# An encoder block planned at build time: turns on SBUF, table loads and a GpSimd delay enter the planner, and GpSimd adds the fourth square of the first head group

## The chip, the cores and the metric

The kernel runs on one core of a Trainium2 chip. A core has five engines with instruction queues of their own: TensorE (PE in the profile), VectorE (DVE), ScalarE (ACT), GpSimd (POOL) and SyncE (SP). They share an on-chip memory, SBUF; matmul results go to PSUM, of which the kernel uses eight banks. The metric is the device time of one execution in microseconds. The batch is 1, the sequence 512, the model width 1024, all in float32.

## The reference

One layer of a streaming encoder. The part that matters here is the mixer: one projection, two groups of eight heads of width 64, each group normalised by itself, and one output projection.

```python
h = rms_norm(x, g_mix_pre)
q_f, k_f, v_f, f_logit, q_c, k_c, v_c = split(h @ w_in)
log_f = log_sigmoid(f_logit + b_fgate)
# group A, forgetting attention: logit[t,s] = q_t.k_s / 8 + c_t - c_s, c = cumsum(log_f), s <= t
o_f = fox_attention(q_f, k_f, v_f, log_f)
# group B: a 64-token chunk sees itself and the 8 chunks before, with a learned relative bias
o_c = chunked_rel_attention(q_c, k_c, v_c, rel_bias)
o_f = rms_norm(o_f.reshape(B, S, 512), g_fox_out)      # over the whole group
o_c = rms_norm(o_c.reshape(B, S, 512), g_chunk_out)
x = x + rms_norm(concat([o_f, o_c]) @ w_out, g_mix_post)
x = x + rms_norm(memory_cross_attention(rms_norm(x), rms_norm(mem)), g_mem_post)
x = x + rms_norm(swiglu(rms_norm(x), w_gate_up, w_down), g_ffn_post)
```

## The kernel before

Every float32 product is made of three passes (`mm3`, lines L410, L411, L413 by the kind of pass): an operand is split into a rounded part `hi` and the rest `lo`. For a weight block, ACT casts it to `hi` (L392) and DVE subtracts to get `lo` (L393): 128 partitions x 1024 elements, both inputs in SBUF. Raw blocks come in on SP's DMA queue.

**Stages.** First the normalisation statistics and the value projections (to 30 us), then the heads, 16 of them in four groups `n` = 0 to 3 (`n` 0 and 1 are side 0, the FoX group A; 2 and 3 are side 1, the chunked group B), beside the projections of the next groups, the first half of the output projection (tile `mix`) and the products of the memory tokens (to 260 us), then cross-attention (to 390 us) and the feed-forward part (to the end).

**One head** runs over four query blocks of 128, the i-th with (i+1) x 128 keys (`head`): two score matmuls (L796, L797) into a PSUM bank `ps_s`; DVE adds the bias and takes the row's bound in one custom instruction (L800, two records in the profile, in the order of instructions `ISA`); ACT takes the exponential and sums it (L810); DVE makes the reciprocal (L811) and scales the row `p` (L812, one input, in SBUF); PE transposes `p` into a bank `ps_t` (L815); ACT rounds the transposed block to `pth` (L817) and DVE subtracts to get `ptl` (L818). At a head's end PE multiplies with the values (L824). Names in the text: `p5_2` is head 5, block 2, written `p_2` with a number in the order of instructions.

**A pair of heads** fills one tile `o`, 128 x 512. `pair_out` scales and splits it on ACT (`oh`, L836) and DVE (`ol`, L837), and GpSimd squares it: the first pair of a group into a tile `sq` (L841), the later ones in place (L843) with an add into `sq` (L845), except the last pair of the group, whose square stays a tile of its own. `group_rs` then sums over the partitions with one-column matmuls (L851), four per tile of squares, and rstd follows on DVE (L856, L417) and GpSimd (L418). GpSimd also masks the FoX biases (L767), adds the squares of the memory tokens (L888) and issues a few DMAs.

**What sets the order.** All instructions of the stages above up to the feed-forward part are recorded first, and then `planned_order` puts them in a fixed order per engine. It simulates each engine with a duration for each instruction (`duration`), a delay from one engine's end to another's start (`SIGNAL`, `TO_PE`, `LANDED`), the dependences, and the buffers of each tile's tag; whenever an engine comes free, the instruction that has the best priority of those that can start is taken. `later(n)` shifts that priority, and `urge` holds such shifts for the four head groups. The rest of the kernel is in the order in which it is written. In the planner as it is, engines touch each other by dependences alone: nothing is held up by another engine's use of a memory, and an `ACT_TABLE_LOAD`, which the compiler puts ahead of an activation whose function is not in the table at hand, costs nothing.

In cross-attention the probabilities of a head are transposed, cast by ACT (`pt`, L1085) and split by DVE (L1086) before PE multiplies them with the values (`ps_o`). After the last head an activation with Silu on one column (L1100) loads the table that the feed-forward part needs; the weight blocks of the output product are cast around it (`woh`, L392).

Of the kernel before, what the change touches and what calls it, by code (L numbers as in the profile page):

```python
# [10 lines left out]
AF = mybir.ActivationFunctionType  # L11
# [24 lines left out]
ENGINES = mybir.EngineType  # L36
# [5 lines left out]
    (ENGINES.DVE, ENGINES.Pool): 80.0, (ENGINES.Activation, ENGINES.Pool): 67.0,  # L42
    (ENGINES.Pool, ENGINES.DVE): 36.0, (ENGINES.Pool, ENGINES.Activation): 34.0,
}
TO_PE, LANDED = 350.0, 60.0


def number(dims):
    n = 1
    for d in dims:  # L50
        n *= d[1]
    return n
# [37 lines left out]
def planned_order(tc, instructions, homes):  # L90
# [35 lines left out]
    def duration(i):  # L126
        kind = type(i).__name__
        n = number(list(i.outs[0].bass_ap.ap)[1:])
        read = [number(list(a.bass_ap.ap)[1:]) for a in i.ins if tile_of(a)]
        columns = sum(n > 8 and m == 1 for m in read)  # L130
        if i.engine == ENGINES.PE:
            return MATMUL * n + 2.0 if n > P else NARROW
        if i.engine == ENGINES.Activation:
            return (284.0 if len(i.outs) > 1 else 160.0) + 0.838 * n + 80.0 * columns
        if i.engine == ENGINES.Pool:
            if n <= 8:
                return 174.0 if kind == "InstTensorCopy" else 1450.0 if n == 1 else 1040.0
            if kind == "InstTensorTensor" and tile_of(i.ins[0]) != tile_of(i.ins[1]):
                return 25.0 + 4.1 * n
            return 25.0 + (0.96 if kind == "InstMemset" else 2.0) * n  # L140
        if kind == "InstCustomDveAnt":
            return 245.0 + 0.99 * n
        if kind == "InstTensorReduce":
            return 158.0 + 1.02 * read[0]
        if kind == "InstMemset":
            return 70.0 + 0.8 * n
        if kind == "InstReciprocal" or n < 8:
            return 158.0
        full = [a for a in i.ins if tile_of(a) and number(list(a.bass_ap.ap)[1:]) > 8]
        if len(full) < 2 and not any(map(in_psum, full)):  # L150
            return 213.0 + 0.526 * n
        return 150.0 + 1.046 * n + 60.0 * columns

    def halves(i):
        starts = []
        for a in [i.outs[0]] + list(i.ins):
            ap = getattr(a, "bass_ap", None)
            if ap is not None and ap.ap[0][1] >= 8:
                whole = number([(0, n) for n in list(ap.tensor.shape)[1:]]) if tile_of(a) else 0
                starts.append(ap.offset // whole if whole else 0)  # L160
        return (starts + starts + [0, 0])[:2]

    nodes = [i for i in instructions if type(i).__name__ not in ("BassTilePoolBoundary", "InstRegisterMove")]
# [38 lines left out]
    for line in after:  # L202
        for k in line:
            missing[k] += 1

    ready, at = {}, [0.0] * len(nodes)
    for k, i in enumerate(nodes):
        if not missing[k]:
# [3 lines left out]
    def reached(e, other, transfer):  # L212
        if e == other and not transfer:
            return 20.0 if e == ENGINES.PE else -20.0
        return TO_PE if other == ENGINES.PE else LANDED if transfer else SIGNAL.get((e, other), 40.0)

    def may_start(k):
        t = at[k]
# [18 lines left out]
    while any(ready.values()):  # L237
        best = None
        for e, waiting in ready.items():
            starts = [(t, k) for t, k in ((may_start(k), k) for k in waiting) if t is not None]  # L240
            if not starts:
                continue
            now = max(free.get(e, 0.0), min(starts)[0])
            able = [(k, t) for t, k in starts if t <= now + 1.0]
            if e == ENGINES.PE:
                alike = [x for x in able if narrow[x[0]] == after_narrow and (after_narrow or x[1] <= now)]
                late = [x for x in able if narrow[x[0]] and x[1] + patience[x[0]] <= now]
                able = alike if after_narrow and alike else late or alike or able
            if best is None or (now, str(e)) < best[:2]:
                best = now, str(e), e, *min(able)  # L250
        _, _, e, k, t = best
        ready[e].remove(k)
        i, start = nodes[k], max(free.get(e, 0.0), t)
        transfer = type(i).__name__ == "InstDMACopy"
        if transfer:
            free[e] = start + ISSUE
            end = landed[e] = max(start + 1900.0, landed.get(e, 0.0)) + 4 * number(i.outs[0].bass_ap.ap) / 300.0
            if e == ENGINES.Pool:
                end += 1500.0
        elif e == ENGINES.PE:  # L260
            cost = duration(i) + (0.0 if narrow[k] or not after_narrow else SUMMED if summed else TURNED)
            after_narrow, summed = narrow[k], number(list(i.outs[0].bass_ap.ap)[1:]) <= 8
            waited = t > free.get(e, 0.0) + 5.0 and cost > 100.0
            free[e] = start + cost + (95.0 if waited else 0.0)
            end = start + max(cost, 60.0) + 170.0
        else:
            if halves(i) != place.get(e, [0, 0]):
                start = max(start, ends.get(e, 0.0) + 28.0)
            place[e] = halves(i)
            end = ends[e] = start + duration(i)  # L270
            free[e] = max(start + 20.0, end - TAIL[e])
        order.setdefault(e, []).append(i)
        for name in used[k]:
            if name not in lasts:
                lasts[name] = {}
                room[homes.tiles[name]].pop(0)
            lasts[name][e, transfer] = end
            uses[name] -= 1
            if not uses[name]:
                room[homes.tiles[name]].append(name)  # L280
        for j, in_turn in after[k].items():
            other = nodes[j].engine
            at[j] = max(at[j], start if in_turn else (start if e == other == ENGINES.PE else end) + reached(e, other, transfer))
            missing[j] -= 1
            if not missing[j]:
                ready.setdefault(other, []).append(j)
# [15 lines left out]
def hybrid_block_kernel(  # L302
# [195 lines left out]
    with tc.tile_pool(name="mix", bufs=1, reuse_waits="tile") as bp:  # L498
# [374 lines left out]
        sqs = []  # L873
        rs_g = []
        order = [(0, g) for g in fox_order] + [(1, 0), (1, 1)]
        for n, (side, g) in enumerate(order):
            with later(-20):
                q, kt, kl, v = group_proj(f"{side}{g}")
            if n == 3:
                mT = big.tile([P, 2, KB, NMEM], F32R, tag="sB", name="mT")  # L880
                mm = bp.tile([P, KB, NMEM], F32, tag="V", name="mm", bufs=2)
                nc.gpsimd.dma_start(mm, mem_t.rearrange("(k p) n -> p k n", p=P))
                msq = bp.tile([P, 4, NMEM], F32, tag="T", name="msq", bufs=3)
                for k in range(0, KB, 2):
                    b = msq[:, 2 * (k > 0) : 2 * (k > 0) + 2, :]
                    act.activation(b, mm[:, k : k + 2, :], AF.Square, scale=1.0 / 32.0)
                    if k:
                        pool.tensor_tensor(out=msq[:, 0:2, :], in0=msq[:, 0:2, :], in1=b, op=ALU.add)  # L888
            if n == 0:
                gate = forget_gate()  # L890
                oh = ox.tile([P, 8, SEQ], F32R, tag="x1", name="oh")
                ol = ox.tile([P, 8, SEQ], F32R, tag="x2", name="ol")
            if n % 2 == 0:
                sqs.append([bp.tile([P, SEQ], F32, tag="sq", name=f"sq{side}", bufs=1)])
            if n == 2:
                with later(300):
                    rs_g.append(group_rs(sqs[0], "rsg0"))
            for b in range(2):
                pr = 2 * g + b
                o = bp.tile([P, SEQ], F32, tag="o", name=f"o{side}{pr}", bufs=2)  # L900
                for h in range(2):
                    hh = 2 * pr + h
                    if n == 3 and 2 * b + h == 1:
                        mem_norm()
                    with later(urge[n] - 295):
                        bias = fox_bias(hh, *gate) if side == 0 else chunk_bias(hh)
                    with later(urge[n]):
                        head(q[b], kt[b], kl[b], v, 2 * b + h, h, bias, o)
                with later(urge[n]):
                    pair_out(  # L910
                        o, (G_FOX, G_CHK)[side] + pr, oh[:, 4 * side + pr, :], ol[:, 4 * side + pr, :],
                        sqs[side][0], n % 2 == 0 and b == 0, n % 2 == 1 and b == 1,
                    )
                if n % 2 == 1 and b == 1:
                    sqs[side].append(o)

        mix = big.tile([P, NT, D], F32, tag="sA", name="mix")
# [899 lines left out]
```

## Time and profile before

| | |
|---|---|
| median of 3 runs | 757.11 us (757.09 to 757.48) |
| profiled execution | 757.56 us, of which the span of the profile 755.8 |
| PE busy | 744.0 us, 98% of the span, 5032 instructions |
| DVE busy | 603.1 us, 80% |
| ACT busy | 445.3 us, 59% |
| GpSimd busy | 59.3 us, 8%, 101 instructions |

The profile times every instruction of one execution. The median is of three executions without it, so an argument made in the profile's numbers is made against 757.56, and 0.45 is between that and the median. A busy PE can still be slow, but here its granted clock is full throughout, so what is lost on PE shows as gaps between its matmuls.

### The profile page before, as it was taken

To read this page: it belongs to the slowest core of one execution; us is meant where nothing else is said; L and a number is where in the kernel's file an instruction comes from. 1 tells how busy PE (TensorE), PEld (TensorE's weight loads), DVE (VectorE), ACT (ScalarE), POOL (GpSimd) and SP (SyncE) were. 2 spreads that over 40 slices of the span, in tenths; PEclk is the share of its full clock that TensorE was granted. 3 is DMA by queue.
4 is the path that set the end of the run, shared out by engine and by line. 5 is a ranking of instruction groups with operands and counts; after the bars stand their busy time and mean duration, and the time that the engine had idled before them with its cause. 6 is when DMAs were issued, how large, how long until landed. Compare 5 with 4: busy or idle time off the path is not lost.

```text
span 755.8 us, 12990 instructions
## 1 busy us (share of the span) xinstructions
PE 744.0 (98%) x5032; PEld 679.8 (90%) x5032; DVE 603.1 (80%) x1101; ACT 445.3 (59%) x817; POOL 59.3 (8%) x101
## 2 busy tenths in 40 slices
PE   9999999999999999999999999999999999999996
PEld 9988887898789988888878999999999999999995
DVE  8669999798788688445654698999989999998756
ACT  8569998686776458344554445666555557544321
POOL 1001232102201211000001200000000000000001
PEclk9999999999999999999999999999999999999999
DMA  7623233324214725411440023333333322243223
GB/s 254 168 81 97 73 88 112 112 71 144 67 57 138 277 75 181 137 57 56 142 145 21 29 97 105 110 110 112 113 112 112 112 85 84 84 139 113 85 84 111
DMA packets 62204, 82.16 MB, mean 109 GB/s; under 512 B 2872, under 2 KB 44344, under 8 KB 62144
## 3 DMA queue, kind: packets, MB, share of 16 engines
q1 hardware_dynamic: 60432, 76.34, 31.8%
q0 software_dynamic: 1280, 4.72, 1.8%
q8 instruction: 39, 0.64, 0.3%
q10 hardware_dynamic: 432, 0.29, 0.1%
q14 instruction: 21, 0.17, 0.1%
HBM read 79.22 MB, written 2.11 MB: 108 GB/s over the span
## 4 chain that ended last, share of the span: by engine, by line
PE 89%; ACT 5%; DVE 3%; issue 1%; DMA 1%; POOL 0%; POOLq 0%; DVEq 0%; ACTq 0%
PE ps_a L410 13%; PE ps_a L411 13%; PE ps_a L413 13%; PE ps_t L1400 3%; PE ps_t L1397 3%; PE ps_t L1398 3%; PE ps_s L1398 3%; PE ps_s L1400 3%; PE ps_s L1397 3%; PE ps_s L410 3%; PE ps_s L413 3%; PE ps_s L411 3%; PE ps_o L824 2%; PE ps_t L815 2%; PE ps_a L1400 1%; PE ps_a L1397 1%
## 5 line engine op out<-in xcount | busy, mean ns | idle before, releaser
L393 DVE TENSOR_TENSOR lo<-raw,hi 128x1024 fp32r<-128x1024 f32 x56 | 69.9, 1258 | 21.1 <-ACT hi L392 13.8
L413 PE MATMUL ps_a<-hTh,lo 128*128 128x512 f32 x192 | 76.2, 397 | 0.0
L411 PE MATMUL ps_a<-hTl,hi 128*128 128x512 f32 x192 | 76.2, 397 | 0.0
L410 PE MATMUL ps_a<-hTh,hi 128*128 128x512 f32 x192 | 75.8, 395 | 0.0
L392 ACT CAST hi<-raw 128x1024 fp32r<-128x1024 f32 x56 | 57.5, 1047 | 30.3 <-PE ps_a L411 20.4
L1193 DVE TENSOR_TENSOR ring_lo<-sums,ring_hi 128x1024 fp32r<-128x1024 f32 (+1 forms) x39 | 46.6, 1195 | 11.8 <-ACT ring_hi L1192 7.2
L1192 ACT CAST ring_hi<-sums 128x1024 fp32r<-128x1024 f32 (+1 forms) x39 | 40.2, 1030 | 16.5 <-PE ps_s L1398 16.5
L1192 ACT CAST ring_hi<-fraw 128x1024 fp32r<-128x1024 f32 (+1 forms) x26 | 26.5, 1032 | 33.6 <-DVE fraw L1279 17.5
L810 ACT ACTIVATE p<-p,nm 128x128 f32<-128x128 f32 (+1 forms) x64 | 36.0, 562 | 11.1 <-DVE nm L800 10.4
L413 PEld LDWEIGHTS ps_a<-hTh,lo 128*128 128x128 f32 x192 | 36.1, 188 | 6.5
L411 PEld LDWEIGHTS ps_a<-hTl,hi 128*128 128x128 f32 x192 | 36.1, 188 | 6.2
L410 PEld LDWEIGHTS ps_a<-hTh,hi 128*128 128x128 f32 x192 | 36.2, 188 | 6.2
L1193 DVE TENSOR_TENSOR ring_lo<-fraw,ring_hi 128x1024 fp32r<-128x1024 f32 (+1 forms) x26 | 30.9, 1199 | 11.3 <-ACT ring_hi L1192 11.3
L818 DVE TENSOR_TENSOR ptl<-ps_t,pth 128x128 fp32r<-128x128 f32 (+1 forms) x64 | 30.4, 483 | 1.7 <-ACT pth L817 1.5
L817 ACT CAST pth<-ps_t 128x128 fp32r<-128x128 f32 (+1 forms) x64 | 26.7, 420 | 8.3 <-PE ps_t L815 7.7
L815 PE MATMUL ps_t<-ident,p 128*128 128x128 f32 x160 | 28.1, 273 | 2.0 <-DVE p L812 2.0
L812 DVE TENSOR_SCALAR p<-p,rc 128x128 f32<-128x128 f32 (+1 forms) x64 | 28.3, 442 | 0.1
L1398 PE MATMUL ps_a<-b,ring_hi 128*128 128x256 f32 x92 | 25.5, 277 | 0.0
L815 PEld LDWEIGHTS ps_t<-ident,p 128*128 128x128 f32 x160 | 19.8, 140 | 6.4 <-issue 1.7
L1397 PE MATMUL ps_a<-b,ring_hi 128*128 128x256 f32 x92 | 25.5, 277 | 0.0
L1400 PE MATMUL ps_a<-b,ring_lo 128*128 128x256 f32 (+1 forms) x93 | 25.5, 276 | 0.0
L410 PE MATMUL ps_a<-hi,oh 128*128 128x512 f32 x64 | 25.3, 396 | 0.0
(572 smaller groups left out, 2774.6 us busy)
## 6 DMA issues: line engine op xcount, KB each, us to landing
raw<-in_dram SPq DMA_DIRECT2D x64, 512.0 KB, 3.7
fraw<-in_dram SPq DMA_DIRECT2D x26, 512.0 KB, 3.5
place<-in_dram SPq DMA_DIRECT2D x21, 512.0 KB, 4.3
more_room<-in_dram SPq DMA_DIRECT2D x15, 512.0 KB, 4.0
row<-gate_rows SPq DMA_DIRECT2D x8, 256.0 KB, 3.2
cb<-in_dram SPq DMA_DIRECT2D x8, 256.0 KB, 2.6
xo<-in_dram POOLq DMA_DIRECT2D x4, 512.0 KB, 7.5
rawv<-in_dram SPq DMA_DIRECT2D x3, 520.0 KB, 6.3
```

Source lines behind the costliest of these rows:

```text
L392: act.copy(hi[:, j : j + n, :], raw)
L393: dve.tensor_tensor(out=lo[:, j : j + n, :], in0=raw, in1=f32(hi[:, j : j + n, :]), op=ALU.subtract)
L410: pe.matmul(dst, sh, mh, start=first, stop=False)
L411: pe.matmul(dst, sh, ml, start=False, stop=False)
L413: pe.matmul(dst[:, to], sl, mh[:, to], start=False, stop=last)
L810: act.activation(p[:, :n], p[:, :n], AF.Exp, bias=nm, scale=-1.0, accum_out=sm)
L815: pe.transpose(tp[:, k * P : (k + 1) * P], p[:, k * P : (k + 1) * P], ident)
L1192: act.copy(h2, v)
L1193: dve.tensor_tensor(out=l2, in0=v, in1=f32(h2), op=ALU.subtract)
L1397: pe.matmul(dst, w[0][:, k, :], b[:, 0, k, :], start=first and k == 0, stop=False, skip_group_check=more)
L1398: pe.matmul(dst, w[0][:, k, :], b[:, 1, k, :], start=False, stop=False, skip_group_check=more)
L1400: pe.matmul(dst[:, to], w[1][:, k, :], b[:, 0, k, to], start=False, stop=last and k == 3, skip_group_check=more,)
```

## The change

Four things change in the planner, and one in the kernel. `TO_PE`, the delay from an engine's end to PE's start, becomes 900 ns for GpSimd (350 before, as for the others still). An activation whose function is Exp, Ln or Silu, and not the last of these three used, starts 1283 ns later. GpSimd's operation on two tiles is taken as 25 + 2.46 ns per element (4.1 before; at 512 elements 1285 ns for 2124). DVE and GpSimd take turns: an instruction of either with 64 or more elements and no large input in PSUM (`shares`) ends later by what is left of the other engine's last such instruction.

In the kernel, the last pair of side 0 is no longer left out of the add: its square is added to `sq0` by GpSimd like those before, and `group_rs` sums one tile of squares for group A, not two. Group B is as it was.

```diff
-TO_PE, LANDED = 350.0, 60.0
+TO_PE, LANDED = {ENGINES.Pool: 900.0, ENGINES.DVE: 350.0, ENGINES.Activation: 350.0}, 60.0
+TABLES = (AF.Exp, AF.Ln, AF.Silu)
+HOLDS = {ENGINES.DVE: 140.0, ENGINES.Pool: 170.0}
...
             if kind == "InstTensorTensor" and tile_of(i.ins[0]) != tile_of(i.ins[1]):
-                return 25.0 + 4.1 * n
+                return 25.0 + 2.46 * n
...
+    def shares(i):
+        n = number(list(i.outs[0].bass_ap.ap)[1:])
+        return n >= 64 and not any(in_psum(a) for a in i.ins if tile_of(a) and number(list(a.bass_ap.ap)[1:]) >= 64)
+
+    table = [AF.Exp]
+    alone, port = [i.engine in HOLDS and shares(i) for i in nodes], {}
...
-        return TO_PE if other == ENGINES.PE else LANDED if transfer else SIGNAL.get((e, other), 40.0)
+        return TO_PE.get(e, 350.0) if other == ENGINES.PE else LANDED if transfer else SIGNAL.get((e, other), 40.0)
...
             place[e] = halves(i)
+            if getattr(i, "func", None) in TABLES and i.func != table[0]:
+                start, table[0] = start + 1283.0, i.func
             end = ends[e] = start + duration(i)
+            if e in HOLDS and alone[k]:
+                end = ends[e] = end + max(0.0, max(port.get(x, 0.0) for x in HOLDS if x != e) - start)
+                port[e] = end - HOLDS[e]
             free[e] = max(start + 20.0, end - TAIL[e])
...
                     pair_out(
                         o, (G_FOX, G_CHK)[side] + pr, oh[:, 4 * side + pr, :], ol[:, 4 * side + pr, :],
-                        sqs[side][0], n % 2 == 0 and b == 0, n % 2 == 1 and b == 1,
+                        sqs[side][0], n % 2 == 0 and b == 0, n == 3 and b == 1,
                     )
-                if n % 2 == 1 and b == 1:
+                if n == 3 and b == 1:
                     sqs[side].append(o)
```

The added lines put the kernel's body 13 lines lower: L812 is L825 in the changed kernel, L851 is L864. The planner's new numbers move several hundred instructions by a few places. Three places are shown; in each the rows are one engine's instructions in order.

The first place is in head 5, at 101 us. `p_2_1232` is its block 2, `ps_t_1240` the bank that takes its transposes, `ps_a` a projection. DVE before:

```order
L812 TENSOR_SCALAR p_1_1216<-p_1_1216,rc_1219 128x256
L393 TENSOR_TENSOR lo_1583<-raw_0_1584,hi_1582 128x1024
L811 RECIPROCAL rc_1235<-sm_1234 128x1
L818 TENSOR_TENSOR ptl_407<-ps_t_1224,pth_406 128x2x128
L812 TENSOR_SCALAR p_2_1232<-p_2_1232,rc_1235 128x384
L800 ISA p_3_1249,nm_1250<-ps_s_1246,row_1177 128x512
```

DVE in the changed kernel:

```order
L825 TENSOR_SCALAR p_1_1216<-p_1_1216,rc_1219 128x256
L406 TENSOR_TENSOR lo_1584<-raw_0_1585,hi_1583 128x1024
L831 TENSOR_TENSOR ptl_407<-ps_t_1224,pth_406 128x2x128
L824 RECIPROCAL rc_1235<-sm_1234 128x1
L813 ISA p_3_1249,nm_1250<-ps_s_1246,row_1177 128x512
L813 ISA nm_1250 128x1
L825 TENSOR_SCALAR p_2_1232<-p_2_1232,rc_1235 128x384
```

The bias step of block 3 has come ahead of the scaling of block 2. PE before, around the transposes of that block:

```order
L413 MATMUL ps_a_1645<-hi_1098,hTl 128x256
L815 MATMUL ps_t_1240<-ident,p_2_1232 128x128 x3
L410 MATMUL ps_a_1645<-hi_1098,hTh 128x256
L411 MATMUL ps_a_1645<-lo_1099,hTh 128x256
L413 MATMUL ps_a_1645<-hi_1098,hTl 128x256
L796 MATMUL ps_s_1312<-T_1135,Q_1061 128x256
L797 MATMUL ps_s_1312<-L_420,Q_1061 128x256
```

PE in the changed kernel:

```order
L426 MATMUL ps_a_1646<-hi_1098,hTl 128x256
L809 MATMUL ps_s_1312<-T_1135,Q_1061 128x256
L810 MATMUL ps_s_1312<-L_420,Q_1061 128x256
L423 MATMUL ps_a_1646<-hi_1098,hTh 128x256
L828 MATMUL ps_t_1240<-ident,p_2_1232 128x128 x3
L424 MATMUL ps_a_1646<-lo_1099,hTh 128x256
```

The transposes have gone from row 554 of PE's list to row 569, behind twelve more projection matmuls, the next score pair and one matmul more.

The second place is the group sum of group A, at 141 us. `o_1379` is the last pair of that group, `sq_618` the tile of squares. GpSimd before:

```order
L782 MEMSET cb_2113 64x64
L843 TENSOR_TENSOR o_1379<-o_1379 128x512
L418 TENSOR_TENSOR rsg_1862<-rsg_1862,mhalf 128x4
L782 MEMSET cb_2479 64x64
L782 MEMSET cb_2581 64x64
```

GpSimd in the changed kernel:

```order
L795 MEMSET cb_2110 64x64
L856 TENSOR_TENSOR o_1379<-o_1379 128x512
L858 TENSOR_TENSOR sq_618<-sq_618,o_1379 128x512
L431 TENSOR_TENSOR rsg_1859<-rsg_1859,mhalf 128x4
L795 MEMSET cb_2476 64x64
```

PE before, the last two of the seven one-column matmuls and what follows:

```order
L851 MATMUL ps_t_1851<-ones,sq_618 128x1
L851 MATMUL ps_t_1851<-ones,o_1379 128x1
L411 MATMUL ps_a_1816<-hTl,hi_1698 128x512
L413 MATMUL ps_a_1816<-hTh,lo_1699 128x512
L796 MATMUL ps_s_1869<-T_1809,Q_1735 128x256
```

PE in the changed kernel, at its one-column matmuls:

```order
L426 MATMUL ps_a_2206<-hi_1773,hTl 128x256
L423 MATMUL ps_a_2206<-hi_1773,hTh 128x256
L864 MATMUL ps_t_1852<-ones,sq_618 128x1 x4
L424 MATMUL ps_a_2206<-lo_1774,hTh 128x256
L426 MATMUL ps_a_2206<-hi_1773,hTl 128x256
```

GpSimd has one add more; PE's matmuls are four instead of eight, at row 786 of its list. Before, one stood at row 703 and seven at rows 741 to 747, right after the projection into the bank `ps_a_1816`; now the four follow the next score pairs and 40 matmuls of the next projection.

The third place is the end of cross-attention, at 377 us. ACT before:

```order
L1067 ACTIVATE xp_4140,xsm_4185<-ps_s_4171,xnm_4184,mix_rs 128x256 x2
L1085 CAST pt<-ps_t_4162 128x2x256
L1100 ACT_TABLE_LOAD
L1100 ACTIVATE mix_ms<-xsm_4185 128x1
L392 CAST woh<-raw_6_4250 128x1024
L1085 CAST pt<-ps_t_4192 128x2x256
L1095 CAST oT_3645<-ps_o_4201 128x512
```

ACT in the changed kernel:

```order
L1080 ACTIVATE xp_4137,xsm_4182<-ps_s_4168,xnm_4181,mix_rs 128x256 x2
L1098 CAST pt<-ps_t_4159 128x2x256
L1113 ACT_TABLE_LOAD
L1113 ACTIVATE mix_ms<-xsm_4182 128x1
L1098 CAST pt<-ps_t_4189 128x2x256
L405 CAST woh<-raw_6_4247 128x1024
L1108 CAST oT_3642<-ps_o_4198 128x512
```

The last cast of `pt` has gone ahead of the weight cast; the table load stays where it was.

Of the places not shown, four are spoken of below. At 124 us DVE's scaling of p8_0 goes ahead of two subtractions L818. At 198 to 202 us the transposes of p13_1 go behind a score matmul and three 512-wide matmuls, those of p13_2 behind three. Near 230 us the second half of a weight subtraction L393 goes ahead of the output's L837, and the score matmul of block 2 of head 16 goes behind the transposes of p15_3. Near 40 us the steps of the forget gate's scan and copy come a few places later on DVE and PE; on SP the loads of one FoX row and two chunk biases move by one place, and on GpSimd the power of the second group's rstd goes ahead of the copies and DMAs of `xo`, the residual.

## The prediction

> **What bounds the kernel now.** I read the page first (engine busy times, the chain that ended last), then the waits of TensorE, then the windows around each wait, and last the timelines of the engines named there.
>
> ```profile
> PE 744.0 (98%) x5032; PEld 679.8 (90%) x5032; DVE 603.1 (80%) x1101; ACT 445.3 (59%) x817; POOL 59.3 (8%) x101
> PE 89%; ACT 5%; DVE 3%; issue 1%; DMA 1%; POOL 0%; POOLq 0%; DVEq 0%; ACTq 0%
> ```
>
> TensorE (PE) is busy for 744.0 of 755.8 us, and the chain that ended last runs over it for 89%. So an edit is worth what it takes from PE's own list or from PE's few stalls. PE's waits, all of them of 0.2 us or more:
>
> ```profile
> PE ps_t L815 <- DVE p L812: 2.0, 3, 0.9
> PE ps_t L509 <- DVE ones L347: 1.1, 1, 1.1
> PE ps_o L410 <- ACT pt L1085: 0.8, 1, 0.8
> PE ps_s L796 <- DVE nm L800: 0.7, 1, 0.7
> PE ps_t L851 <- POOL o L843: 0.2, 1, 0.2
> ```
>
> All but L509 (the start) lie in the planned part, and windows show how local they are (second number: PE busy, of 10 us; then weight loads, DVE, ACT, POOL):
>
> ```profile
> 100.00:110.00 10.00, 9.14 (x70) 8.56 (x69) 9.92 (x31) 8.83 (x23) 1.86 (x4) 1.00 0.48 132
> 120.00:130.00 10.00, 9.38 (x50) 7.45 (x49) 9.43 (x28) 8.71 (x20) 3.36 (x7) 1.00 0.32 100
> 190.00:200.00 10.00, 9.47 (x45) 7.45 (x44) 7.66 (x16) 9.16 (x19) 2.58 (x2) 1.00 0.35 108
> 230.00:240.00 10.00, 9.28 (x74) 8.90 (x73) 9.76 (x26) 6.89 (x15) 0.54 (x1) 1.00 0.45 153
> 376.00:386.00 10.00, 9.18 (x43) 7.15 (x42) 4.14 (x8) 4.37 (x8) 0.00 (x0) 1.00 0.48 146
> ```
>
> The granted clock is 1.00 in all five, so a lost tenth there is a wait and no slower matmul.
>
> **Stall 1, at 101.** The next fence holds rows of the DVE, POOL and PE timelines (start, duration, in brackets the idle time before) and the group row of L393 (min/median/max).
>
> ```profile
> 98.25 0.35 DVE L812 TENSOR_SCALAR p<-p,rc 128x256 f32<-128x256 f32 x1
> 98.84 2.25 DVE L393 TENSOR_TENSOR lo<-raw,hi 128x1024 fp32r<-128x1024 f32 x1 [0.24 <-ACT hi L392]
> 101.41 0.40 DVE L812 TENSOR_SCALAR p<-p,rc 128x384 f32<-128x384 f32 x1
> ...
> 98.72 1.29 POOL L845 TENSOR_TENSOR sq<-sq,o 128x512 f32<-128x512 f32 x1
> ...
> 100.71 0.28 PE L411 MATMUL ps_a<-lo,hTh 128*128 128x256 f32 x1
> 100.83 0.28 PE L413 MATMUL ps_a<-hi,hTl 128*128 128x256 f32 x1
> 101.97 0.52 PE L815 MATMUL ps_t<-ident,p 128*128 128x128 f32 x3 [0.86 <-DVE p L812]
> ...
> L393 DVE TENSOR_TENSOR lo<-raw,hi x56: 1198/1220/2304, 20.2 to 368.4; 128x1024 fp32r<-128x1024 f32 x56
> ```
>
> GpSimd's add of squares starts at 98.72, a DVE subtraction with both inputs in SBUF starts 0.12 later and takes 2.25 instead of 1.22: it stood for 1.03 of the add's 1.29. The scaling of p (L812) queued behind it, and the transposes behind that. PE's starts lie 1.14 apart (100.83 to 101.97) where a 256-wide matmul takes 0.12 (100.71 to 100.83): the stall costs 1.02, that is the 0.86 of the bracket and 0.16 more. I add the same 0.16 to the other brackets.
>
> **Stalls 2, 4 and 5** have the same cause with other victims; stall 5 is the 2.3 us L393 again.
>
> ```profile
> 123.50 1.10 DVE L812 TENSOR_SCALAR p<-p,rc 128x128 f32<-128x128 f32 x1
> ...
> 123.15 1.28 POOL L845 TENSOR_TENSOR sq<-sq,o 128x512 f32<-128x512 f32 x1
> ...
> 124.75 0.30 PE L815 MATMUL ps_t<-ident,p 128*128 128x128 f32 x1 [0.62 <-DVE p L812]
> ...
> 198.43 1.47 DVE L812 TENSOR_SCALAR p<-p,rc 128x256 f32<-128x256 f32 x1
> ...
> 198.45 1.29 POOL L888 TENSOR_TENSOR msq<-msq 128x512 f32<-128x512 f32 x1 [0.78 <-ACT msq L886]
> ...
> 199.95 0.44 PE L815 MATMUL ps_t<-ident,p 128*128 128x128 f32 x2 [0.53 <-DVE p L812]
> ...
> 229.32 2.30 DVE L393 TENSOR_TENSOR lo<-raw,hi 128x1024 fp32r<-128x1024 f32 x1
> ...
> 229.26 1.28 POOL L845 TENSOR_TENSOR sq<-sq,o 128x512 f32<-128x512 f32 x1
> ...
> 232.04 0.41 PE L796 MATMUL ps_s<-T,Q 128*128 128x384 f32 x1 [0.72 <-DVE nm L800]
> ```
>
> An L812 of 256 columns took 0.35 at 98.25 and 1.47 at 198.43 beside GpSimd. With 0.16 each the three stalls are 0.78, 0.69 and 0.88.
>
> **Stall 3 (140.7) and stall 6 (379.9)** are of another kind:
>
> ```profile
> 139.12 1.54 POOL L843 TENSOR_TENSOR o<-o 128x512 f32<-128x512 f32 x1 [7.63 <-DVE ol L837]
> ...
> 139.94 0.39 PE L413 MATMUL ps_a<-hTh,lo 128*128 128x512 f32 x1
> 140.16 0.39 PE L410 MATMUL ps_a<-hTh,hi 128*128 128x512 f32 x1
> 140.72 0.38 PE L851 MATMUL ps_t<-ones,o 128*128 128x1 f32 x2 [0.16 <-POOL o L843]
> 142.30 0.48 PE L411 MATMUL ps_a<-hTl,hi 128*128 128x512 f32 x1
> ...
> 376.30 0.58 ACT L1085 CAST pt<-ps_t 128x512 fp32r<-128x512 f32 x1
> 376.90 1.28 ACT L1100 ACT_TABLE_LOAD   x1
> 378.19 0.20 ACT L1100 ACTIVATE mix_ms<-xsm 128x1 f32<-128x1 f32 x1
> 378.30 1.03 ACT L392 CAST woh<-raw 128x1024 fp32r<-128x1024 f32 x1
> 379.24 0.58 ACT L1085 CAST pt<-ps_t 128x512 fp32r<-128x512 f32 x1
> 379.87 0.50 PE L410 MATMUL ps_o<-pt,vm 128*128 128x512 f32 x1 [0.82 <-ACT pt L1085]
> ```
>
> In stall 3 PE, which starts a 512-wide matmul every 0.22 to 0.23 (139.94, 140.16), waits 0.16 + 0.16 = 0.32 for the last square, then issues seven of the eight one-column matmuls of the group (the first stands alone earlier): (142.30 - 140.72) / 7 = 0.226 each. In stall 6 the table load of 1.28 delays ACT, the weight cast L392 comes up first, and the cast of pt that PE waits for stands behind it: 0.82 + 0.16 = 0.98.
>
> **The change, part by part** (lines of before; in the changed kernel all these are 13 higher).
>
> *Group sum.* Four of eight L851 matmuls go: 4 x 0.226 = 0.90 off PE's own list, with nothing to hide it. In exchange GpSimd makes one more add, 1.28 (its row at 123.15), with the row of L851 now behind it. Is that late? The multiply started at 139.12; stalls 1 and 2 and one L851 now gone from ahead of it put it near 137.1; 1.54 + 1.28 give 139.9; if one subtraction L393 takes its turn first, 141.1; two, 142.4. PE reaches the four matmuls after 40 256-wide ones (0.117 each, 4.7) and two score pairs (4 x 0.117 = 0.5) behind the place that it reached at 140.39 before, and 2.0 earlier: 143.6. The margin is 1.2 to 3.7, so the 0.32 goes too, and GpSimd's 900 ns to PE is inside it. DVE's L856 now waits for those matmuls with all of head 9's softmax queued behind it: it is free near 144.6, p9_0 needs, by my estimate from L812's 0.35 and the operations like it, 2 us more, and PE has 26 matmuls (3 us) before its transposes.
>
> *Turns on SBUF, and the shorter add.* Stall 1: the add and the L393 still collide, I take the 2.25 as staying. But the transposes stand 15 matmuls later (15 x 0.117 = 1.75), so PE comes to them at about 102.7. On DVE the order is now L818, L800, L812, which puts p some 0.6 later than 101.81, with 0.16 to PE: 102.6. Gone, with 0.1 to spare. Stall 2: L812 goes ahead of the 0.69 subtraction L818, hence to about 122.9, before the add at 123.15. Gone. Stall 4: the transposes move behind 3 x 0.227 + 0.117 = 0.80 of matmuls, against 0.69. Gone, by 0.1. Its neighbour, a 0.2 wait for the next p at 202.1, I leave standing. Stall 5: the second half of L393 goes ahead of the output's L837, whose result starts GpSimd, and the score matmul goes eight rows later, behind the transposes of p15_3. Gone. What is late next there: the add then meets the first L393 of the next weights. If GpSimd issues first, DVE gives p16_0 about 1.2 later than otherwise, against some 0.7 of cover: 0 to 0.9 lost; I take 0.45, since the two starts are too close to call.
>
> *Table load in the plan.* The cast of pt goes ahead of L392. It would run from 378.3 to 378.9, the second half of it on DVE (L1086) follows 0.7 later; PE's first matmul on it would come at 378.9 as before the stall. Up to 0.1 may remain; stall 6 goes. The displaced weight half is read on PE some 30 512-wide matmuls later (30 x 0.22 = 6.6), so its delay of 0.6 is hidden.
>
> The Trainium skill, "ScalarE: Activation LUTs", section "What ACT_TABLE_LOAD costs", prices a switch of tables at about 2.7 us with a drain of 1.4 beside the load. By that rule pt would be 1.4 later and the sum below 1.0 higher; the rows here speak against it, since the load starts 0.02 after the cast before it ends and the next ACTIVATE follows 0.01 after the load. I give it 3 in 100, inside the forecast's range.
>
> *Everything else that moved* (the gate's scan and copy, the first biases, loads of row3, cb3 and cb6 by one place on SP's queue, rsg1's power ahead of the four xo loads on GpSimd's queue): I cost it at nothing. The first biases have the whole projection before the first head as cover, and xo is read only after the output projection's first blocks. If such a cover failed, the price would be of the order of one wait above, 0.3 to 1.0. I add 0.3 for one of them, or for one of the two 0.1 margins.
>
> *Sum.* 1.02 + 0.78 + 0.32 + 0.69 + 0.88 + 0.98 = 4.67, and 0.90: 5.57 off the profiled execution's 757.56 (its span 755.8, 1.8 around it), 751.99. Back come 0.45 + 0.3: 752.7. That execution is 0.45 above the median of the runs, 757.11, so the median comes to 752.3. About 0.2% (1.5 us) is what a measurement can tell from no change.
>
> **The rivals.** *A: DVE stays the limit where it is full.* DVE is busy 9.92 and 9.43 of 10 in the windows of stalls 1 and 2, and 9.76 in that of stall 5. Moving PE's work cannot speed it up; where the add still blocks it, the lost time turns up behind another p. Then only the table load, the four matmuls and stall 3's 0.32 hold: 0.98 + 0.90 + 0.32 = 2.2, time 754.9 (754.0 to 756.5). Against it: of DVE's time in these windows about 1.0, 0.8 and 1.1 are the blocked part itself, and PE has projection matmuls to put in between.
>
> *B: The waits only move.* As A, and the new add brings one collision of its own of 1.28 with its 0.16: 2.2 - 1.4 = 0.8, time 756.3 to 757.1, no change that can be told.
>
> *C: Slower: fillers run out.* The plan spends projection matmuls earlier as cover for late transposes. If the last heads before 250 then stand without any, each quarter of a head brings a wait like those above, which mean (1.02 + 0.78 + 0.69 + 0.88) / 4 = 0.84. It decides at nine bare quarters (7.6 against 5.57 + 1.5): 757.1 - 5.6 + 7.6 = 759.1. The order speaks against it: in the changed kernel 256-wide matmuls still stand between all transposes of heads 15 and 16.
>
> **How the numbers follow.** The forecast, most covers hold, 0.64, with its own range of 751.0 (nothing comes back, and small waits such as that at 202.1 go too) to 753.7 (three covers miss by 0.3 to 0.9). A 0.20, B 0.08, C 0.08. Faster by over 0.2%, below 755.6, is the forecast and most of A: 0.79; within 0.2% the rest of A and B: 0.13; slower 0.08. The range goes from 751.0 to 755.6 and leaves out C, B and the slow end of A.
>
> **What the profile of the changed kernel would show.** Waits: "ps_t <- DVE p" down from 2.0 to 0.5 or less, the rows for pt and nm gone, none for the group sum. Windows: PE at 9.8 or more in 100 to 110 and in 120 to 130, and 9.9 in 376 to 386. The one-column group of squares with half the records for the first group, L845 five times at 1.28. L393 may still show 2.3: then the gain came from the new places of the transposes and not from fewer collisions. I am wrong if PE shows new brackets of over 0.5 in 100 to 250 (A or B), above all for p16_0, or a row of them before 250 (C).

## The result, and the profile after

The changed kernel takes 750.68 us (median of 4 executions, 750.3 to 751.43), the kernel before on the same chip 757.3: a ratio of 0.9913, 95% interval 0.9896 to 0.993. The forecast of 752.3 had the direction and the larger part of the size (4.8 below the 757.11 that it started from, where 6.6 came); its range of 751.0 to 755.6 begins 0.3 us too high. The profiled execution is the fastest of the four (750.3, span 748.5), and that of before one of its slower ones, so the two spans differ by 7.3 where the medians differ by 6.6.

The page of the changed kernel, busy times and the chain that ended last:

```profile
PE 740.4 (99%) x5024; PEld 679.0 (91%) x5024; DVE 602.4 (80%) x1101; ACT 445.1 (59%) x817; POOL 63.4 (8%) x102
PE 98%; issue 0%; DVE 0%; DMA 0%; ACT 0%; POOLq 0%; POOL 0%; DVEq 0%; ACTq 0%
```

The chain runs over PE for 98% of the span, before for 89%. PE has eight records less (a one-column matmul is two). All of PE's waits that the view lists, and three of its windows:

```profile
PE ps_t L522 <- DVE ones L360: 1.0, 1, 1.0
PE ps_s L423 <- DVE vhi L568: 0.4, 1, 0.4
...
100.00:110.00 10.00, 10.00 (x71) 9.29 (x70) 9.80 (x28) 9.18 (x23) 2.23 (x4) 1.00 0.49 132
120.00:130.00 10.00, 10.00 (x54) 8.48 (x53) 9.79 (x27) 9.82 (x23) 3.88 (x8) 1.00 0.39 96
230.00:240.00 10.00, 10.00 (x83) 9.74 (x83) 8.37 (x19) 5.60 (x11) 0.00 (x0) 1.00 0.45 148
```

Both waits are at the start, in the first 6 us. In the planned part none is left: PE is busy for all of the windows in which it lost 0.86, 0.62 and 0.72 before. In the first two DVE is as full as it was (9.80 and 9.79 of 10, before 9.92 and 9.43), so a full DVE did not hold PE up there.

Is the collision gone? The DVE, GpSimd and PE timelines of the changed kernel at the place of stall 1:

```profile
98.72 2.24 DVE L406 TENSOR_TENSOR lo<-raw,hi 128x1024 fp32r<-128x1024 f32 x1 [0.25 <-ACT hi L405]
101.88 0.41 DVE L825 TENSOR_SCALAR p<-p,rc 128x384 f32<-128x384 f32 x1
...
98.59 1.28 POOL L858 TENSOR_TENSOR sq<-sq,o 128x512 f32<-128x512 f32 x1
...
102.22 0.28 PE L809 MATMUL ps_s<-T,Q 128*128 128x256 f32 x1
102.58 0.49 PE L828 MATMUL ps_t<-ident,p 128*128 128x128 f32 x3
```

It is not. The subtraction takes 2.24 beside the add, as before; p is ready at 102.29, and PE comes to the transposes only at 102.58, with no bracket. At 227 us the same two meet in the other order:

```profile
227.10 1.35 DVE L406 TENSOR_TENSOR lo<-raw,hi 128x1024 fp32r<-128x1024 f32 x1 [0.42 <-ACT hi L405]
...
226.16 1.22 POOL L856 TENSOR_TENSOR o<-o 128x512 f32<-128x512 f32 x1 [22.20 <-DVE ol L850]
227.45 2.16 POOL L858 TENSOR_TENSOR sq<-sq,o 128x512 f32<-128x512 f32 x1
```

Here DVE's instruction was first, and GpSimd's add took 2.16 instead of 1.28. No instruction waits for that add. The adds of before and of the changed kernel (min/median/max) show that this is not the only one:

```profile
L845 POOL TENSOR_TENSOR sq<-sq,o x4: 1282/1288/1293, 98.7 to 229.3; 128x512 f32<-128x512 f32 x4
L858 POOL TENSOR_TENSOR sq<-sq,o x5: 1284/2153/2212, 98.6 to 227.4; 128x512 f32<-128x512 f32 x5
```

Three of the five adds now take 2.15 to 2.21, each behind a DVE subtraction that started first. The prediction expected five of 1.28. So in part the new order lets GpSimd bear the collision, and for its adds nobody waits.

### The profile page after: what moved, and what is told of

The parts are those of the page before. It is cut to its first block, busy times and chain, and to the rows that moved or that the text cites. A ratio compares the mean times of both kernels' runs of the same rounds, so it can differ in the third digit from the quotient of the medians.

```text
span 748.5 us, 12983 instructions
## 1 busy us (share of the span) xinstructions
PE 740.4 (99%) x5024; PEld 679.0 (91%) x5024; DVE 602.4 (80%) x1101; ACT 445.1 (59%) x817; POOL 63.4 (8%) x102
## 4 chain that ended last, share of the span: by engine, by line
PE 98%; issue 0%; DVE 0%; DMA 0%; ACT 0%; POOLq 0%; POOL 0%; DVEq 0%; ACTq 0%
PE ps_a L424 16%; PE ps_a L426 16%; PE ps_a L423 16%; PE ps_t L1413 3%; PE ps_t L1410 3%; PE ps_t L1411 3%; PE ps_s L1411 3%; PE ps_s L1413 3%; PE ps_s L1410 3%; PE ps_s L423 3%; PE ps_s L426 3%; PE ps_s L424 3%; PE ps_o L837 3%; PE ps_t L828 2%; PE ps_a L1410 1%; PE ps_a L1413 1%
## 5 line engine op out<-in xcount | busy, mean ns | idle before, releaser
L825 DVE TENSOR_SCALAR p<-p,rc 128x128 f32<-128x128 f32 (+1 forms) x64 | 25.7, 401 | 0.2
L424 PE MATMUL ps_a<-lo,oh 128*128 128x512 f32 x64 | 25.2, 393 | 0.0
```

What stands on the lines that cost most here:

```text
L424: pe.matmul(dst, sh, ml, start=False, stop=False)
```

## The experiments

Theory: the gain is the sum of PE's stalls and four matmuls; turns on SBUF take away stalls 1, 2, 4 and 5 by putting PE work in front of late results, the table load's price takes stall 6, the fourth square 0.9 and stall 3. Rivals: any new plan shifts collisions at random; or the plan avoids the collisions. Each time is a median, set against the kernel before on the same chip (757.2 to 757.6).

**The square alone.** `pair_out` and `sqs.append` as in the diff, the planner of before.

> Only the fourth square of group A is added by GpSimd; the planner is that of before. Theory (the parts add up): four one-column matmuls go, 4 x 0.226 = 0.90 us, and the 0.32 wait for the last square if the plan moves the group sum far enough; stalls 1, 2, 4, 5 and 6 stay with their brackets: 1.2 below before, about 756.0. Rival (any new plan shifts the collisions at random): stalls 1, 2, 4 and 5 change too, and the time is off 756.0 by more than 0.8 either way.

755.99, 1.40 below 757.39 (ratio 0.9981, 0.9972 to 0.999). PE's waits of this kernel:

```profile
PE ps_t L815 <- DVE p L812: 2.0, 3, 0.9
PE ps_t L509 <- DVE ones L347: 1.1, 1, 1.1
PE ps_o L410 <- ACT pt L1085: 0.8, 1, 0.8
PE ps_s L796 <- DVE nm L800: 0.7, 1, 0.7
```

The row for the group sum is gone and the rest are to a tenth those of before, though about a hundred rows of PE's order had moved. That is 0.9 and 0.32, with 0.2 more; for this edit the random rival falls.

**The table load alone.**

```diff
+            if getattr(i, "func", None) in TABLES and i.func != table[0]:
+                start, table[0] = start + 1283.0, i.func
```

> Only the price of a table load enters the planner (30 rows of PE's order and 2 of ACT's move). Theory: stall 6 goes, 0.98 us, and with it the small wait of 0.31 us at 389 that follows in the same weight block, if that one hangs on it: 1.0 to 1.3 below before. Rival: the switch costs a drain beside the load, and 1.0 of stall 6 stays: no change. The windows of 90 to 250 us should be as before under both.

756.06, 1.33 below (0.9984, 0.9975 to 0.9993). ACT's timeline of this kernel:

```profile
376.89 1.28 ACT L1104 ACT_TABLE_LOAD   x1
378.18 0.20 ACT L1104 ACTIVATE mix_ms<-xsm 128x1 f32<-128x1 f32 x1
378.29 0.57 ACT L1089 CAST pt<-ps_t 128x512 fp32r<-128x512 f32 x1
378.76 1.05 ACT L396 CAST woh<-raw 128x1024 fp32r<-128x1024 f32 x1
```

The cast of pt starts 0.12 after the load ends: no drain shows, and the load takes the 1.28 that the planner now counts. The extra 0.3 is a wait that the prediction had not counted. In the kernel before, PE's starts at 389.57 and 390.11 lie 0.54 apart where a 512-wide matmul takes 0.23: PE waited for ACT to clear a bank. That ACT was late there after stall 6 is read from the runs: every profile that has stall 6 has this gap, and none without it has.

```profile
389.47 1.56 ACT L1137 COPY y<-ps_a 128x512 f32<-128x512 f32 x3
...
389.57 0.39 PE L413 MATMUL ps_a<-woh,oT 128*128 128x512 f32 x1
390.11 0.50 PE L410 MATMUL ps_a<-woh,oT 128*128 128x512 f32 x1
```

In this kernel PE's starts at that place keep their 0.23.

**The turns alone**, the two edits with `HOLDS`, with GpSimd's add still taken for 2.12.

> Only the turns of DVE and GpSimd on SBUF enter the planner, with the old duration of 2.12 us for GpSimd's add. Theory: stalls 1, 2, 4 and 5 go, 1.02 + 0.78 + 0.69 + 0.88 = 3.4 us, so 3.0 to 3.6 below before, with stalls 3 and 6 still there. Rival: the turns are of use only with the right length of the add; with 2.12 for 1.28 the plan puts work at the wrong places, and less than 1.7 of the 3.4 is gained.

753.39, 4.0 below (0.9945, 0.9931 to 0.9958). All of PE's waits for p and for nm are gone, that for the group sum too; stall 6 stays. Its place of stall 4 shows how, and the last two rows the next transposes of the same head:

```profile
196.82 1.46 DVE L821 TENSOR_SCALAR p<-p,rc 128x256 f32<-128x256 f32 x1
...
196.84 1.29 POOL L897 TENSOR_TENSOR msq<-msq 128x512 f32<-128x512 f32 x1 [1.33 <-ACT msq L895]
...
198.44 0.38 PE L824 MATMUL ps_t<-ident,p 128*128 128x128 f32 x2
...
200.07 0.39 PE L422 MATMUL ps_a<-hi,ol 128*128 128x512 f32 x1
200.53 0.52 PE L824 MATMUL ps_t<-ident,p 128*128 128x128 f32 x3
```

The scaling of p is held for 1.46 beside GpSimd's add, as it was before (1.47), and PE's transposes have no bracket. The 4.0 is more than the 3.4 of the four stalls: stall 3 goes as well (0.32), and 0.3 is not assigned. The small wait at 202 stays: PE's starts at 200.07 and 200.53 lie 0.46 apart, 0.23 more than a 512-wide matmul takes. The rival, that the turns need the right length of the add, falls for this plan.

**GpSimd's hold, with the order of before.** The adds touch every eighth column; the planner is told the old durations.

```diff
-                    pool.tensor_tensor(out=sq, in0=sq, in1=o, op=ALU.add)
+                    pool.tensor_tensor(out=sq[:, ::8], in0=sq[:, ::8], in1=o[:, ::8], op=ALU.add)
...
-                        pool.tensor_tensor(out=msq[:, 0:2, :], in0=msq[:, 0:2, :], in1=b, op=ALU.add)
+                        pool.tensor_tensor(out=msq[:, 0:2, ::8], in0=msq[:, 0:2, ::8], in1=b[:, :, ::8], op=ALU.add)
```

> The order of before on all engines, kept by giving the planner the old durations, but GpSimd's adds of squares (L845 and L888) do every eighth column alone and so leave out seven eighths of those sums. Theory (GpSimd's hold of SBUF is the cause, the order only exposes it): DVE's L393 at 99 and 229 us take 1.2 instead of 2.3, L812 at 123.5 and 198.4 under 0.4, and PE's stalls 1, 2, 4 and 5 go: 3.0 to 3.6 us below before with the same order. Rival (the order itself has DVE late, and the collision is incidental): under 1 us is gained.

754.02, 3.37 below (0.9953, 0.9941 to 0.9965), where the four stalls give 3.4. The DVE and GpSimd timelines at stall 1:

```profile
99.28 1.38 DVE L395 TENSOR_TENSOR lo<-raw,hi 128x1024 fp32r<-128x1024 f32 x1 [0.26 <-ACT hi L394]
...
99.14 0.44 POOL L847 TENSOR_TENSOR sq<-sq,o 128x64 f32<-128x64 f32 x1
```

The add of 0.44 costs the subtraction 0.16 where that of 1.29 cost 1.03. The order on PE, DVE, ACT and GpSimd is that of before, row for row, and of the four stalls only 0.17 of the first is left between PE's starts; stalls 3 and 6 stay. So the collisions were the cause of these four. Taking them away, or covering them, are two ways to the same 3.4 us.

**The changed kernel without the turns.**

> The changed kernel without the turns on SBUF: the shorter add, the table load, the 900 ns and the fourth square are in. Theory (parts add up): only the parts measured alone come, 1.40 for the square and 1.33 for the table load, so about 754.6, with PE's waits of 0.5 to 0.9 us for p and for nm still in the list. Rival (the turns are one of several ways to move the transposes, and the length of the add does it too): at least half of the 4.0 us of the turns comes without them, 752.6 or less.

755.62, 1.97 below before's 757.59 (0.997, 0.9959 to 0.9982). The parts would have given 2.7; the profiled execution, at 754.83 one of the two fastest, has the old waits for p and nm and one more, of 0.39 us at 228; why the median lies 0.8 above it is not shown. The turns cannot be replaced by the length of the add.

**The fourth square of group B too.**

```diff
-                        sqs[side][0], n % 2 == 0 and b == 0, n == 3 and b == 1,
+                        sqs[side][0], n % 2 == 0 and b == 0, False,
...
-                if n == 3 and b == 1:
-                    sqs[side].append(o)
```

> The changed kernel, with the fourth square of group B too added by GpSimd, so that group B's sum takes four one-column matmuls and not eight. Theory (PE's list is what counts, GpSimd's add is covered): 4 x 0.226 = 0.9 us below the changed kernel, about 749.8. Rival (near 243 us little stands between the last square and the rows that need its sum): the add of 1.3 to 2.2 us appears as a wait of PE or of DVE, and the time is that of the changed kernel or up to 1.2 us above it.

753.82: 3.1 above the changed kernel (0.9952 of before, 0.9939 to 0.9964), worse than the rival said. The DVE, GpSimd and PE timelines:

```profile
244.37 4.25 DVE L406 TENSOR_TENSOR lo<-raw,hi 128x1024 fp32r<-128x1024 f32 x2 [0.18 <-ACT hi L405]
249.15 0.16 DVE L869 TENSOR_SCALAR gms<-ps_t 128x4 f32<-128x4 f32 x1 [0.54 <-PE ps_t L864]
250.57 1.88 DVE L977 TENSOR_TENSOR kT<-ps_a,kT 128x512 fp32r<-128x512 f32 x3
...
245.38 2.15 POOL L858 TENSOR_TENSOR sq<-sq,o 128x512 f32<-128x512 f32 x1
...
248.16 0.95 PE L864 MATMUL ps_t<-ones,sq 128*128 128x1 f32 x8
251.31 0.50 PE L423 MATMUL ps_a<-hi,oh 128*128 128x512 f32 x1 [2.19 <-DVE kT L977]
```

GpSimd's multiply and add and two subtractions hold each other up (2.15 for the add's 1.28; 4.25 for two of 1.22), DVE's L869 waits for the sum, and the subtractions for kT, which free PE's banks, stand behind it. PE saves 0.9 and waits 2.3. Most of the rest of the loss is the clock:

```profile
248.00:251.30 3.30, 1.11 (x11) 1.02 (x10) 2.73 (x6) 3.01 (x6) 1.78 (x2) 1.00 0.62 234
251.30:252.80 1.50, 1.50 (x6) 1.22 (x7) 1.50 (x3) 0.94 (x1) 1.32 (x5) 0.88 0.91 244
252.80:254.30 1.50, 1.50 (x5) 1.19 (x4) 1.38 (x2) 0.00 (x0) 1.50 (x3) 0.50 1.01 376
256.00:260.00 4.00, 4.00 (x19) 3.33 (x18) 2.16 (x3) 1.20 (x3) 0.00 (x0) 1.00 1.01 399
```

After the wait the granted clock (third number from the end) falls to 0.50 for 3.4 us, from 252.4 to 255.8; matmuls of 0.23 then come every 0.43, and seven of them cost 1.4 more.

**The order of the changed kernel with short adds**, the same edit as above made to it.

> The order of the changed kernel, with GpSimd's adds of squares (L858 and L901) on every eighth column alone, seven eighths of those sums left out. Theory (the plan covers the collisions and does not avoid them): DVE's stretched instructions get shorter, by some 4 us in sum between 90 and 250 us, and the time stays within 0.3 us of the changed kernel, since PE waits for none of them. Rival (what is left of the collisions still costs): 0.5 us or more below the changed kernel.

750.7 (750.37 to 752.15), the changed kernel's 750.68 (0.9906 of before, 0.9891 to 0.9921). DVE's subtraction at stall 1 (L408 here) takes 1.38 instead of 2.24, DVE is busy for 600.1 us instead of 602.4 (some 4 less was expected), and the time does not move: the plan covers what is left of the collisions. The profiled execution is the longest of the four, and shows another wait, at 86 us. DVE's timeline at stall 1, and ACT's at 86:

```profile
100.32 1.38 DVE L408 TENSOR_TENSOR lo<-raw,hi 128x1024 fp32r<-128x1024 f32 x1 [0.25 <-ACT hi L407]
...
86.40 0.40 ACT L781 ACTIVATE fb<-row,ct 128x128 f32<-128x128 f32 x1 [1.60 <-DMA row<-gate_rows]
```

A FoX bias row landed late, ACT waited 1.6 with an exponential queued behind, and PE lost 0.91.

**350 ns from GpSimd to PE again.**

> The changed kernel with 350 ns again from GpSimd to PE (22 rows of PE's order move, all near the group sum). Theory: the sum is covered by more than 0.55 us, so the time stays within 0.3 us of the changed kernel. Rival: the 900 ns is what removed stall 3, and PE waits 0.2 to 0.5 us for the sum of squares.

750.61 (0.9911, 0.9899 to 0.9924): no difference. The 900 ns adds nothing here.

**The changed kernel again, and without the square.**

> The changed kernel as it is, for its spread and a second profile. Theory (in some executions the transfer of one FoX bias row lands late and ACT, then PE wait for it, up to 0.9 us, as in the run with short adds): executions between 750.3 and 752.2, and if the profiled one lies above 751 its trace shows ACT waiting for a row from gate_rows. Rival (the spread is of the whole span): a profiled execution above 751 has no single wait that accounts for it.

> All four edits of the planner, with the last square of group A a tile of its own again (eight one-column matmuls). Theory: the changed kernel plus 4 x 0.226 = 0.9 us, and no wait for the sum, about 751.6; with e1's 1.40 the two ways to measure the square differ by the 0.33 of stall 3, which the planner's edits remove by themselves. Rival (the square's worth is independent of the planner): 1.4 us above the changed kernel, with a wait of 0.2 or more for the group's sum.

The first: 750.71 (750.5 to 750.87; 0.9913, 0.99 to 0.9927), with no wait for a bias row in its profile; no execution was above 751, so it does not test the late row. The second: 751.61, 0.90 above it (0.9925, 0.9913 to 0.9938), and no wait for the sum. So the square is worth 0.9 once the planner's edits are in, and 1.40 without them: stall 3 can be removed by either. The profile without the square has 0.21 of the small wait for p13_2 again (PE's starts near 199.6), so that one is not gone for good.

The parts measured alone, 1.40 + 1.33 + 4.00, give 6.7; stall 3 is in two of them, so 6.4 is left, beside the 6.6 of all together.

**The old length of the add, all else as in the changed kernel.**

> The changed kernel with the old 25 + 4.1 ns per element for GpSimd's add in the planner; the real add stays at 1.29. Theory (a plan that takes the add for longer than it is leaves more cover than needed and loses nothing): within 0.4 us of the changed kernel. Rival (transposes and subtractions are placed by wrong ends of the add): 0.6 us or more above it, with brackets for p in PE's waits.

754.82 (753.09 to 756.11; 0.9958, 0.9944 to 0.9971), so 2.4 above the changed kernel (750.71) at its best and 4.1 in the median: the time is the rival's, and more, but not its sign: PE's one bracket for p comes from a late bias row. By itself this number moves nothing (with the shorter add alone all engines' orders are those of before, row for row), and the turns alone gained their 4.0 with the old length. So the old length hurts only beside the other edits; beside which of them was not run. The profiled execution is the longest, with that row (0.88 lost on PE) and these waits of PE; the last row but one is GpSimd's, the last a window with its clock:

```profile
219.76 0.39 PE L423 MATMUL ps_a<-mT,hi 128*128 128x256 f32 x1 [0.64 <-ACT mT L880]
222.09 0.39 PE L424 MATMUL ps_a<-mT,hi 128*128 128x256 f32 x1 [1.35 <-DVE mT L881]
...
208.34 0.71 POOL L431 TENSOR_TENSOR rm<-rm,mhalf 128x2 f32<-128x2 f32 x1 [7.28 <-DVE rm L430]
...
224.00:226.00 2.00, 2.00 (x9) 1.81 (x8) 1.56 (x6) 1.23 (x3) 0.00 (x0) 0.50 0.22 72
```

The memory tokens' rstd (L431) runs at 208.3, in the changed kernel at 203.2, and everything made from it (mm, mT) is late by about as much. Late alone is not what costs: in the kernel before it runs at 207.0, and no row of PE waits, since PE's first matmul on mT stands at 222.3 there and at 219.8 here. PE loses 2.8 us around these two rows, and its clock falls to 0.50 for 3.4 us from 223.0. Why a longer add gives this plan is open.

**The changed kernel without the table load.**

> The changed kernel without the price of a table load in the planner. Theory (its effect is local, at 377 and 389 us): 1.3 us above the changed kernel, about 752.0, with PE's waits for pt (0.98) and of 0.31 at 388 back and no other. Rival (the price also acts at the two loads near 35 us, whose plan moves the gate steps and, through them, the heads): more than 1.8 us or less than 0.8 us above it, with other waits in 90 to 250 us.

752.33 (0.993, 0.9917 to 0.9944). That is 1.65 above 750.68, but on a chip whose kernel before takes 757.56; measured from there, 5.23 are gained instead of 6.62, so 1.4 is lost. PE's starts show the 0.99 for pt and the 0.31 that follows back, and no other wait in the planned part: 1.3 of the 1.4.

## Why the prediction was right or wrong

- **Stall 1** (1.02): right, with its mechanism. Predicted p at about 102.4 and PE at 102.7, measured 102.29 and 102.58.
- **Stall 2** (0.78): gone, but not as told. L825 did run ahead of GpSimd's add, but it met the multiply of the pair and took 0.93 (122.81 to 123.74); PE comes to its transposes only at 124.81.
- **Stall 3 and the four matmuls** (0.32 + 0.90): right. PE reaches the matmuls at 143.64, predicted 143.6; GpSimd's sum is ready at 142.81, later than the range of 139.9 to 142.4: the multiply started at 139.54, not at 137.1, and the add took 2.15. So the margin was 0.8, not 1.2 to 3.7. The difference of 0.90 came out in the run without the square.
- **Stall 4** (0.69): gone, by another way: the scaling of p13_1 started 0.16 ahead of the add and took 0.35. The cover as told is what the run with the turns alone shows (1.46, and no bracket). The neighbour of 0.2, left standing in the prediction, went too: DVE was first by 0.12 there. Which engine comes first was not forecast, and the run without the square has the wait again, so that is luck.
- **Stall 5** (0.88) and its successor: stall 5 went, and the step that failed is what was put back for it: 0.45, half of 0.9, for the add meeting the next L393. They did meet, but DVE was first by 0.35, and GpSimd bore the delay (2.16). PE has no wait for p16_0: 0 came back.
- **Stall 6** (0.98): right in place and size, and no drain showed, as the rows had said: the run with the table load alone shows the 1.28 of the load and nothing beside it. The Trainium skill ("ScalarE: Activation LUTs", section "What ACT_TABLE_LOAD costs") gives about 2.7 us for a switch; the measurement decides here. Missed was the wait of 0.31 that hung on stall 6.
- **The reserve** of 0.3 for a failed cover: not needed. No cover failed.

So the mechanism was right, and the sum failed in two terms. What comes back was taken as 0.45 + 0.3 = 0.75 and measured 0. And PE's list of waits was taken for all that PE lost beside its own list: the 0.31 at 389 was put at nothing, the 0.2 at 202 left standing. These make 1.3 of the 1.6 us by which the forecast was off, and with them put right the sum gives 751.0, the low end of the range, which had no room for anything more. The last 0.3 to 0.4 (0.6 if one starts from before's 757.3 in this measurement) is not assigned. Gaps of this size come and go near 290 us, at the transposes of `mix`: 0.22 between PE's starts in before's profile, none in the changed kernel's, 0.18 in the run with short adds that has the same order. That they make up the rest is not shown.

Of the rivals, A falls: DVE stays as full where stalls 1 and 2 were, and PE waits for nothing there. B describes what happened in the run with both groups, not in this one. C did not occur.

## What to carry to other kernels

A planner need not avoid a collision: if it knows how long the late result takes, it can put other work in front of its reader, and the collision stays but costs nothing. Price what the planner does not know, and test the prices together: one that alone changes no row (the length of the add) was worth 4.1 us beside the others, though the turns alone did without it. When adding up stalls, look for those that hang on another, and for gaps that the list of waits does not name: its brackets begin only when the last matmul has ended, 0.16 us late, and a bracket of 0.15 (389.57 to 390.11) was not in it.

## What the runs showed of the hardware

With both groups' squares added, a wait of PE of 2.2 us in the list brought the clock down to 0.50 for 3.4 us afterwards and cost 1.4 us on top of itself; just before that wait PE had 0.95 us of one-column matmuls alone. With the old length of the add two waits of 0.64 and 1.35, 3.3 us (218.8 to 222.1) in which PE started two matmuls, did the same. The waits of up to 0.9 us before left the clock at 1.00 in their windows. How much work in how long a time keeps the clock up is not shown. The Trainium skill ("TensorE: Matmul & The Clock Gate", section "Part 1: The HAM clock gate (the "warmup" mystery)") has the clock halved after an idle window of about 3.4 us. The halving agrees; no stretch here was idle for so long.

The same collision of DVE and GpSimd can hold either: 2.24 for DVE with GpSimd 0.13 ahead, 2.16 for GpSimd with DVE 0.35 ahead. The Trainium skill ("SBUF — State Buffer", section "Who interferes with whom") has it that whoever issues first keeps the shared ports for its whole instruction. These rows agree with it.

A single late bias row was worth 0.9 us in two of the twelve experiments' profiles, more than most of the stalls that the plan removed.
